# The front of a three-layer transformer kernel: weights of the first projection by feature chunk, the condition vector broadcast by its transfer, spare products ahead

## The chip, the cores and the metric

The kernel runs as one program on one core of a Trainium2 chip. A core has five engines that work side by side on one on-chip memory: TensorE (PE, matrix products into eight PSUM banks), VectorE (DVE), ScalarE (ACT), GpSimd (POOL), and SyncE (SP), which here issues all DMA transfers. The time is device microseconds of one execution; the kernel before took 1167.01 us, the median of three runs from 1165.86 to 1167.97.

## The reference

256 tokens of 1024 features pass three layers. The first two are modulated by a condition vector `c`; the front of the kernel is concerned with these lines:

```python
mod = jnp.einsum('bd,ldm->lbm', jax.nn.silu(c), w_mod) + b_mod[:, None, :]
for i in range(DEPTH):
    sh_m, sc_m, g_m, sh_f, sc_f, g_f = [t[:, None, :] for t in jnp.split(mod[i], 6, axis=-1)]
    h = x * (1.0 + sc_m) + sh_m
    if i % 2 == 0:
        y = even_mixer(h, cos, sin, w_in_even[i // 2], w_out_even[i // 2])
    else:
        ...
    x = layer_norm(ALPHA * x + (1.0 + g_m) * y, ln_mix_g[i], ln_mix_b[i])
    h = x * (1.0 + sc_f) + sh_f
    y = swiglu(h, w_gate[i], w_up[i], w_down[i])
    x = layer_norm(ALPHA * x + (1.0 + g_f) * y, ln_ffn_g[i], ln_ffn_b[i])
```

`w_mod` is 2 x 1024 x 6144, so `mod` costs 50 MB of reading, 12288 outputs in 96 chunks of 128. `even_mixer` projects `h` by `w_in_even` and runs stick-breaking attention beside a sparse attention that keeps the 64 best keys of every query (top-k over an index score); `odd_mixer` is a differential attention. The third layer is a gated linear recurrence with convolutions and a feed-forward block. All of it is fp32.

## The kernel before

Activations lie with features on the partitions: `Xf[k]` is feature chunk k (128 features x 256 tokens). Weights arrive as slabs of 1024 rows x 256 columns, in two halves of 128 x 1024. `add_plan("w0", 10, WHOLE)` lists the ten slabs of the first projection: the first seven are used as fp32 ("whole"), each half straight from its transfer into a `whi` or `wlo` buffer. All later ones are loaded into `stage`, split into two reduced-precision halves by an ACT copy (`whi`) and a DVE subtraction (`wlo`), and multiplied in three products, which together take less TensorE time than one fp32 product. `mm3` does either.

`mod_chunks(n)` handles the next chunks of `mod`: a transfer of 0.5 MB from `wmod` into an `mst` buffer (three of them; some early pairs go as one 1-MB transfer into `stage`), then one DVE scalar_tensor_tensor that multiplies with `scb` (silu(c), the same 1024 values on every partition) and adds up along the row into `raw`. After chunk pair k the DVE adds the bias, which gives shift and scale of feature chunk k, and ACT forms `Xf[k]` (L921). So the first 16 chunks gate the eight `Xf[k]`, and the first products follow k by k: `min(NST, W0 + W1 * k)` halves are in work at step k, six in all, each catching up from its chunk 0. The next two groups of 16 and 8 chunks feed the scale after the attention and the gate, which the first layer norm needs; the other chunks run beside later stages.

At the very start the vector block `vec` and the identity are loaded, ACT takes silu of the eight columns of `c`, TensorE turns their broadcasts by eight transposes (L512), and ACT copies them to `scb`. At k == 1 the rest of the constants and the positions are loaded and `rope_tables()` (L875) works out the rotary cosines and sines on DVE and ACT. Later on the path: the index scores, eight rounds of top-k on DVE, the mask `biasb`, which TensorE multiplies in by an identity; then attention, output projection, and the first layer norm, whose sums are taken by products with one column (`128x1`) and spread to all partitions by four `128x128` products with `sm`.

All operations are recorded by a `Plan`. Its `order()` simulates the engines with a cost per operation (L178) and places, on every engine and on the DMA queue, the ready operation with the lowest index plus a bias; buffers come from pools in that order. So a change in the front can move instructions anywhere. Since one helper records everything, nearly all rows of the trace carry line L428.

Of the kernel before, what the change touches and what calls it, by code (L numbers as in the profile page):

```python
# [8 lines left out]
F32 = mybir.dt.float32  # L9
# [9 lines left out]
S = 256  # L19
# [5 lines left out]
ALPHA = 4.0 ** 0.25  # L25
# [16 lines left out]
for _name, _w in (("ident", 128), ("tn", 128), ("neg1", 128), ("inv1024", 128),  # L42
                  ("causal", 128), ("strict", 128), ("inv", 1), ("sgn", 1)):
    _C[_name] = _n
    _n += _w
# [14 lines left out]
NST = 6  # L60
W0 = 1
W1 = 2
EACT = 2
WHOLE = 7
ORDER = 0
# [366 lines left out]
def kernel(ctx, tc, io, out):  # L432
# [60 lines left out]
    run.sync.dma_start(vec, io["vecs"])  # L493
    cst = const("cst", NCST)
    run.sync.dma_start(cst[:, :128], io["cst"][:, :128])
# [3 lines left out]
    def C(name, w=128):  # L499
        return cst[:, _C[name]:_C[name] + w]  # L500
# [5 lines left out]
    sc = sm("sc", 8)  # L506
    A.activation(sc, VC("c", 0, 8), AF.Silu)
    scb = const("scb", 1024)
    for i in range(2):
        ps = bank("ps_c")  # L510
        for k in range(4):
            T.transpose(ps[:, k * 128:k * 128 + 128], sc[:, 4 * i + k:4 * i + k + 1].to_broadcast([128, 128]), ident)  # L512
        A.activation(scb[:, i * 512:i * 512 + 512], ps, AF.Copy)
# [20 lines left out]
    def mod_chunks(n, lag=0):  # L534

        for _ in range(n):
# [5 lines left out]
            if 4 <= i < 16 and i % 4 < 2:  # L542
                if i % 4 == 0:
                    mod_chunks.st = run.tile("stage", SL, F32, "mst2").rearrange("p (c n) -> p c n", c=2)
                    run.sync.dma_start(mod_chunks.st, io["wmod"][i:i + 2].rearrange("c p n -> p c n"))
                st = mod_chunks.st[:, i % 4, :]
# [29 lines left out]
    add_plan("w0", 10, WHOLE)  # L576
# [334 lines left out]
    ws, pss = [], [gbank("ps_g") for _ in range((NST + 1) // 2)]  # L911
    for k in range(8):
# [3 lines left out]
        if k == 1:  # L916
            run.sync.dma_start(cst[:, 128:], io["cst"][:, 128:])
        new = len(ws)
        while len(ws) < min(NST, W0 + W1 * k):
            ws.append(take())  # L920
        A.activation(Xf[k], x0[k // 4][:, k % 4, :], AF.Identity, scale=MV(0, 1, k), bias=MV(0, 0, k))  # L921
        for c, w in enumerate(ws):
            for kk in range(0 if c >= new else k, k + 1):
                mm3(pss[c // 2][:, (c % 2) * S:(c % 2) * S + S], w, kk, X, kk, ALLT, kk == 0 and c % 2 == 0, kk == 7)
        if k == 1:
            rope_tables()
    if WHOLE < 10:
        for k in range(8):
            split(X[0][k], X[1][k], Xf[k])
    ps = bank("ps_s")  # L930
    for k in range(8):
        T.matmul(ps[:, :S], C("inv1024"), x0[k // 4][:, k % 4, :], start=k == 0, stop=k == 7)
    xm = w1("xm")[:, :S]
    A.activation(xm, ps[:, :S], AF.Copy, scale=ALPHA)
# [799 lines left out]
def lay_out(inputs):  # L1734
# [40 lines left out]
    cst[:, _C["inv1024"]:_C["inv1024"] + 128] = 1.0 / 1024  # L1775
# [84 lines left out]
```

## Time and profile before

| | us |
|---|---|
| median of three runs | 1167.01 |
| profiled execution | 1165.6 |
| its span on the core | 1163.8 |
| TensorE busy | 1132.3 (97%) |
| VectorE busy | 910.6 (78%) |
| ScalarE busy | 723.5 (62%) |

The span is what the trace covers; 1.8 us of the execution lie around it. Busy time of TensorE comes from records of passes: an fp32 product with 256 columns is two passes, so a row "x8" of these holds four products. "Granted clock" is the share of its full speed that the chip allowed TensorE, as a mean over the window; over the whole span it was 0.988.

### The profile page before, as it was taken

Reading aid. Unit: us, or ns where it says so; the run is one execution under the profiler, and the core shown is the slowest. Engines: PE = TensorE matmul, PEld = TensorE weight load, DVE = VectorE, ACT = ScalarE, POOL = GpSimd, SP = SyncE. Lnnn points to the kernel's source line nnn. Section 1 sums busy time; section 2 is a strip of 40 time slices with the busy share of each in tenths; the row PEclk is TensorE's granted clock in tenths of the full one; section 3 lists DMA queues with packets and bytes.
Section 4 is the critical chain, followed back from the end, with each engine's and each line's share of the span. In section 5 each row is a group of like instructions: output and inputs, shape, how many; then the busy total and the mean of one; then the engine's idle time right before and its main releaser. Section 6 shows DMA issues by size and latency. Waiting matters only on the chain.

```text
span 1163.8 us, 22183 instructions
## 1 busy us (share of the span) xinstructions
PE 1132.3 (97%) x8835; PEld 1083.9 (93%) x8835; DVE 910.6 (78%) x1686; ACT 723.5 (62%) x1312; POOL 88.2 (8%) x84
## 2 busy tenths in 40 slices
PE   5999999999999899999999999999999999999997
PEld 4885899999999778999999999999999999999996
DVE  6799899888999999865557886996669887866642
ACT  3558676445449887764455558786767865655541
POOL 0110200000231302000003400000000010000011
PEclk9999989999999999899999999999999999999998
DMA  9938758988995333455554634344433424555441
GB/s 353 409 131 309 240 196 319 337 325 305 335 335 191 114 129 126 145 218 184 187 191 168 228 110 158 130 148 179 155 117 131 178 87 171 195 188 193 169 163 37
DMA packets 42247, 232.28 MB, mean 200 GB/s; under 512 B 4640, under 2 KB 6176, under 8 KB 24096
## 3 DMA queue, kind: packets, MB, share of 16 engines
q1 hardware_dynamic: 42144, 230.87, 55.0%
q8 instruction: 69, 1.13, 0.4%
q14 instruction: 34, 0.28, 0.1%
HBM read 229.81 MB, written 1.05 MB: 198 GB/s over the span
## 4 chain that ended last, share of the span: by engine, by line
PE 85%; DVE 7%; DMA 3%; ACT 3%; issue 1%; DVEq 0%; SPq 0%; ACTq 0%
PE pa L428 85%; DVE w L428 4%; ACT w L428 2%; DVE wlo L428 2%; DMA mst<-in_wmod_dram 1%; DVE sm L428 1%; DVE mst L428 1%; DMA whi<-in_w_dram 1%; DMA cst<-in_cst_dram 1%; ACT whi L428 1%; DMA vec<-in_vecs_dram 0%; ACT sm L428 0%; ACT scb L428 0%; DVE lnv0lmg L428 0%; DVEq L1856 0%
## 5 line engine op out<-in xcount | busy, mean ns | idle before, releaser
L428 PE MATMUL pa<-w,whi 128*128 128x256 f32 (+4 forms) x5104 | 914.5, 287 | 9.6 <-DMA whi<-in_w_dram 7.5
L428 PEld LDWEIGHTS pa<-w,whi 128*128 128x128 f32 x5104 | 766.9, 190 | 17.0 <-ACT w L428 7.6
L428 PE MATMUL pa<-w,wlo 128*128 128x256 f32 (+3 forms) x2608 | 659.5, 289 | 0.0
L428 ACT ACTIVATE whi<-stage 128x1024 fp32r<-128x1024 f32 (+1 forms) x330 | 340.2, 1042 | 257.2 <-PE pa L428 233.9
L428 DVE TENSOR_TENSOR wlo<-stage,whi 128x1024 fp32r<-128x1024 f32 (+1 forms) x330 | 401.4, 1226 | 110.1 <-ACT whi L428 104.5
L428 PEld LDWEIGHTS pa<-w,wlo 128*128 128x128 f32 x2608 | 464.0, 190 | 7.7 <-issue 4.0
L428 ACT ACTIVATE w<-w 128x256 fp32r<-128x256 f32 (+9 forms) x257 | 117.6, 470 | 74.0 <-DVE w L428 70.3
L428 ACT ACTIVATE w<-pa 128x256 f32<-128x256 f32 (+12 forms) x298 | 108.3, 391 | 40.9 <-PE pa L428 36.1
L428 DVE TENSOR_TENSOR w<-w,w 128x256 fp32r<-128x256 f32 (+7 forms) x263 | 120.1, 474 | 8.0 <-ACT w L428 5.1
L428 DVE SCALAR_TENSOR_TENSOR mst<-mst,scb 128x1024 f32<-128x1024 f32 x90 | 109.5, 1226 | 10.8 <-DMA mst<-in_wmod_dram 10.6
L428 DVE TENSOR_TENSOR w<-w,pa 128x256 f32<-128x256 f32 (+2 forms) x146 | 58.9, 417 | 57.3 <-PE pa L428 52.3
L428 POOL TENSOR_TENSOR w<-w,w 128x256 f32<-128x256 f32 (+1 forms) x50 | 56.5, 1150 | 527.5 <-ACT w L428 320.7
L427 ACT ACT_TABLE_LOAD x59 | 75.7, 1283 | 1.7 <-PEq L1850 0.7
L428 PE MATMUL pa<-w,w 128*128 128x128 f32 (+8 forms) x340 | 70.0, 331 | 1.7 <-DVE w L428 1.1
L428 PEld LDWEIGHTS pa<-w,w 128*128 128x128 f32 (+4 forms) x340 | 41.4, 171 | 11.5 <-issue 4.1
L428 PE MATMUL pa<-cst,w 128*128 128x1 f32 (+4 forms) x284 | 46.5, 265 | 3.6 <-DVE w L428 2.2
L428 PEld LDWEIGHTS pa<-cst,w 128*128 128x128 f32 (+2 forms) x284 | 36.0, 175 | 12.0 <-ACT w L428 4.5
L428 POOL TENSOR_TENSOR w<-w 128x256 f32<-128x256 f32 x4 | 3.2, 799 | 415.2 <-DVE w L428 415.2
L428 PE MATMUL pa<-w 128*128 128x128 f32 x240 | 34.6, 274 | 0.0
L428 PE MATMUL pa<-whi,w 128*128 128x512 f32 x96 | 32.5, 417 | 0.2 <-ACT w L428 0.2
L428 PEld LDWEIGHTS pa<-w 128*128 128x128 f32 x240 | 31.2, 191 | 0.0
L428 DVE SCALAR_TENSOR_TENSOR w<-pa,vec,w 128x256 f32<-128x256 f32 (+1 forms) x48 | 23.1, 482 | 6.7 <-PE pa L428 5.7
(145 smaller groups left out, 537.1 us busy)
## 6 DMA issues: line engine op xcount, KB each, us to landing
mst<-in_wmod_dram SPq DMA_DIRECT2D x90, 512.0 KB, 5.4
stage<-in_wgu_dram SPq DMA_DIRECT2D x44, 1024.0 KB, 4.9
stage<-in_wi_dram SPq DMA_DIRECT2D x36, 1024.0 KB, 4.8
stage<-in_wup_dram SPq DMA_DIRECT2D x22, 1024.0 KB, 4.8
stage<-in_wd_dram SPq DMA_DIRECT2D x24, 896.0 KB, 4.7
stage<-in_w_dram SPq DMA_DIRECT2D x15, 1024.0 KB, 6.2
stage<-in_wo_dram SPq DMA_DIRECT2D x12, 1024.0 KB, 4.8
stage<-in_wd_dram SPq DMA_DIRECT2D x12, 1024.0 KB, 4.8
```

What stands on the lines that cost most here:

```text
L427: self.nc.scalar.preload_act_table_set(tables[i])
L428: fn(*[real(a) for a in args], **{k: real(a) for k, a in kw.items()})
```

## The change

The condition vector comes by a transfer that repeats its 4 KB on all 128 partitions (512 KB written), and ACT takes silu of the 128 x 1024 result in place; the eight transposes and two copies go. `vec` arrives in two parts, its first 104 columns early, the rest after the loop. The constants `1/1024` are set by GpSimd and no longer loaded. TensorE runs twelve fp32 products of a tile of ones into a bank that nobody reads.

The first four slabs lie in a new array `w0k` by feature chunk: at step k two transfers of 128 x 512 (256 KB each) bring the chunk's rows of all eight column blocks, and TensorE multiplies these eight with `Xf[k]`. The sums of x (`inv1024` products) are spread over the steps. The 1-MB transfers of chunk pairs move from even to odd k (four instead of three). The constants and the rotary tables move from k == 1 to k == 5.

```diff
-NST = 6
-W0 = 1
-W1 = 2
+NK = 8
+NWARM = 12
...
-    run.sync.dma_start(vec, io["vecs"])
+    scb = const("scb", 1024)
+    c_ap = io["cvec"]
+    run.sync.dma_start(scb, bass.AP(tensor=c_ap.tensor, offset=c_ap.offset, ap=[[0, 128], [1, 1024]]))
+    run.sync.dma_start(vec[:, :104], io["vecs"][:, :104])
     cst = const("cst", NCST)
-    run.sync.dma_start(cst[:, :128], io["cst"][:, :128])
+    inv1024 = const("inv1024", 128)
+    G.memset(inv1024, 1.0 / 1024)
+    wt = w2("wt")
+    V.memset(wt, 1.0)
+    ps = bank("ps_w")
+    for i in range(NWARM):
+        T.matmul(ps[:, :S], wt[:, :128], wt[:, :S], start=True, stop=True)
...
-    sc = sm("sc", 8)
-    A.activation(sc, VC("c", 0, 8), AF.Silu)
-    scb = const("scb", 1024)
-    for i in range(2):
-        ps = bank("ps_c")
-        for k in range(4):
-            T.transpose(ps[:, k * 128:k * 128 + 128], sc[:, 4 * i + k:4 * i + k + 1].to_broadcast([128, 128]), ident)
-        A.activation(scb[:, i * 512:i * 512 + 512], ps, AF.Copy)
+    A.activation(scb, scb, AF.Silu)
...
-            if 4 <= i < 16 and i % 4 < 2:
-                if i % 4 == 0:
+            if i < 16 and i % 4 >= 2:
+                if i % 4 == 2:
...
-    add_plan("w0", 10, WHOLE)
+    add_plan("w0", 10 - NK // 2, WHOLE - NK // 2)
...
-        if k == 1:
-            run.sync.dma_start(cst[:, 128:], io["cst"][:, 128:])
-        new = len(ws)
-        while len(ws) < min(NST, W0 + W1 * k):
-            ws.append(take())
+        wk = []
+        for a in range(2):
+            w = run.tile("wlo" if a else "whi", HW, F32, "whole")[:, :NK * 64]
+            run.sync.dma_start(w, io["w0k"][k][:, a * NK * 64:(a + 1) * NK * 64])
+            wk += [w[:, j * 128:j * 128 + 128] for j in range(NK // 2)]
         A.activation(Xf[k], x0[k // 4][:, k % 4, :], AF.Identity, scale=MV(0, 1, k), bias=MV(0, 0, k))
-        for c, w in enumerate(ws):
-            for kk in range(0 if c >= new else k, k + 1):
-                mm3(pss[c // 2][:, (c % 2) * S:(c % 2) * S + S], w, kk, X, kk, ALLT, kk == 0 and c % 2 == 0, kk == 7)
-        if k == 1:
+        for c in range(NK):
+            T.matmul(pss[c // 2][:, (c % 2) * S:(c % 2) * S + S], wk[c], Xf[k], start=k == 0 and c % 2 == 0, stop=k == 7,
+                     skip_group_check=True)
+        if k % 2:
+            for kk in (k - 1, k):
+                T.matmul(ps_x, C("inv1024"), x0[kk // 4][:, kk % 4, :], start=kk == 0, stop=kk == 7)
+        if k == 5:
+            run.sync.dma_start(cst, io["cst"])
             rope_tables()
+    run.sync.dma_start(vec[:, 104:], io["vecs"][:, 104:])
```

What the planner makes of it shows in the order of instructions. On VectorE before, the rotary tables (from the CAST of the positions in `w` to `cosT`) stand around the first pair of chunks from `stage`, the pair of k = 2:

```order
L428 CAST w_1_217<-w_0_201 128x256
L428 TENSOR_SCALAR w_1_217<-w_1_217,cst_100 128x256
L428 TENSOR_SCALAR w_2_224<-w_1_217 128x256
L428 TENSOR_SCALAR w_2_224<-w_2_224 128x256 x2
L428 SCALAR_TENSOR_TENSOR w_1_217<-w_2_224,w_1_217 128x256 x3
L428 TENSOR_SCALAR w_1_217<-w_1_217 128x256
L428 SCALAR_TENSOR_TENSOR stage_203,raw_185<-stage_203,scb_169 128x1024 x2
L428 TENSOR_TENSOR mod_193<-raw_185,bm_131 128x2
L428 TENSOR_TENSOR w_3_239<-w_3_239 128x256
L428 TENSOR_SCALAR cosT_262<-w_3_239 128x256
L428 CAST strib_264<-cst_100 128x128
L428 CAST causb_266<-cst_100 128x128
```

After the change they stand behind the third of these pairs, that of k = 5 (`stage_233`), and ahead of the chunks of k = 6 (`mst`):

```order
L427 SCALAR_TENSOR_TENSOR stage_233,raw_154<-stage_233,scb_101 128x1024 x2
L427 TENSOR_TENSOR mod_170<-raw_154,bm_143 128x2
L427 CAST identb_302<-cst_254 128x128
L427 CAST strib_304<-cst_254 128x128
L427 CAST causb_307<-cst_254 128x128
L427 CAST w_1_309<-w_0_261 128x256
L427 TENSOR_SCALAR w_1_309<-w_1_309,cst_254 128x256
L427 TENSOR_SCALAR w_2_314<-w_1_309 128x256
L427 TENSOR_SCALAR w_2_314<-w_2_314 128x256 x2
L427 SCALAR_TENSOR_TENSOR w_1_309<-w_2_314,w_1_309 128x256 x3
L427 TENSOR_SCALAR w_1_309<-w_1_309 128x256
L427 SCALAR_TENSOR_TENSOR mst_264,raw_154<-mst_264,scb_101 128x1024
```

With them moved the three casts of constants. Ahead of the scales for the first layer norm (`mod` with 16 columns) VectorE before runs chunks (`mst`) and evictions of products (`w<-pa,w`), and no splitting of weights:

```order
L428 SCALAR_TENSOR_TENSOR mst_1078,raw_185<-mst_1078,scb_169 128x1024
L428 SCALAR_TENSOR_TENSOR mst_1118,raw_185<-mst_1118,scb_169 128x1024
L428 SCALAR_TENSOR_TENSOR mst_1138,raw_185<-mst_1138,scb_169 128x1024
L428 TENSOR_TENSOR w_18_1062<-pa_1172,w_4_1059 128x256
L428 SCALAR_TENSOR_TENSOR w_13_1170<-pa_1030,w_13_1170 128x512
L428 SCALAR_TENSOR_TENSOR w_13_1170<-pa_1066,w_13_1170 128x256
L428 SCALAR_TENSOR_TENSOR mst_1157,raw_185<-mst_1157,scb_169 128x1024
L428 SCALAR_TENSOR_TENSOR mst_1174,raw_185<-mst_1174,scb_169 128x1024
L428 SCALAR_TENSOR_TENSOR mst_1190,raw_185<-mst_1190,scb_169 128x1024
L428 TENSOR_TENSOR mod_193<-raw_185,bm_131 128x16
```

After the change six of the subtractions that make `wlo` stand there, of the first feed-forward slabs, and the last two chunks behind or between them:

```order
L427 SCALAR_TENSOR_TENSOR mst_1199,raw_154<-mst_1199,scb_101 128x1024
L427 TENSOR_TENSOR wlo_1263<-stage_899,whi_1244 128x1024
L427 TENSOR_TENSOR wlo_1277<-stage_899,whi_1255 128x1024
L427 TENSOR_TENSOR wlo_1293<-stage_989,whi_1271 128x1024
L427 TENSOR_TENSOR wlo_1309<-stage_989,whi_1283 128x1024
L427 TENSOR_TENSOR wlo_1321<-stage_1050,whi_1299 128x1024
L427 SCALAR_TENSOR_TENSOR mst_1213,raw_154<-mst_1213,scb_101 128x1024
L427 TENSOR_TENSOR wlo_1351<-stage_1050,whi_1332 128x1024
L427 SCALAR_TENSOR_TENSOR mst_1220,raw_154<-mst_1220,scb_101 128x1024
L427 TENSOR_TENSOR mod_170<-raw_154,bm_143 128x16
```

Those six moved ahead of the scales. On TensorE before, the one-column sums of the first layer norm (`128x1`, ten rows of two, the last six here) follow each other, and products with feed-forward weights (258 columns) begin behind them:

```order
L428 MATMUL pa_1457<-cst_100,w_11_1396 128x1 x2
L428 MATMUL pa_1457<-cst_100,w_2_1424 128x1 x2
L428 MATMUL pa_1457<-cst_100,w_11_1396 128x1 x2
L428 MATMUL pa_1457<-cst_100,w_1_1455 128x1 x2
L428 MATMUL pa_1457<-cst_100,w_11_1396 128x1 x2
L428 MATMUL pa_1457<-cst_100,w_3_1476 128x1 x2
L428 MATMUL pa_1496<-w_5_1259,whi_1357 128x258
L428 MATMUL pa_1496<-w_0_1263,whi_1357 128x258
L428 MATMUL pa_1496<-w_5_1259,wlo_1382 128x258
```

After the change feed-forward products run ahead of the sums and among them:

```order
L427 MATMUL pa_1437<-w_5_1399,wlo_1321 128x258
L427 MATMUL pa_1478<-inv_0_99,w_7_1421 128x1 x2
L427 MATMUL pa_1431<-w_5_1399,whi_1271 128x258
L427 MATMUL pa_1454<-w_5_1399,whi_1332 128x258
L427 MATMUL pa_1478<-inv_0_99,w_8_1427 128x1 x2
L427 MATMUL pa_1478<-inv_0_99,w_14_1425 128x1 x2
L427 MATMUL pa_1478<-inv_0_99,w_0_1457 128x1 x2
L427 MATMUL pa_1478<-inv_0_99,w_14_1425 128x1 x2
L427 MATMUL pa_1478<-inv_0_99,w_2_1469 128x1 x2
L427 MATMUL pa_1478<-inv_0_99,w_14_1425 128x1 x2
```

So 37 of these 258-column products instead of 15 stand ahead of the four that spread the norm's results.

## Rows read from the trace of the kernel before

**Rows 1.** The page, first part: busy us, share of the span, instructions of TensorE.

```profile
PE 1132.3 (97%) x8835; PEld 1083.9 (93%) x8835; DVE 910.6 (78%) x1686; ACT 723.5 (62%) x1312; POOL 88.2 (8%) x84
```

**Rows 2.** What TensorE waited for in the span: us in total, times, longest.

```profile
PE pa L428 <- DMA whi<-in_w_dram: 7.5, 3, 4.5
```

**Rows 3.** Timeline of TensorE: start, duration, passes, idle before and its releaser.

```profile
3.33 1.95 PE L428 MATMUL pa<-cst,sm 128*128 128x128 f32 x8 [3.33 <-ACT sm L428]
9.80 1.19 PE L428 MATMUL pa<-w,whi 128*128 128x256 f32 x2 [4.52 <-DMA whi<-in_w_dram]
13.56 1.22 PE L428 MATMUL pa<-w,whi 128*128 128x256 f32 x2 [2.57 <-DMA whi<-in_w_dram]
...
49.59 3.62 PE L428 MATMUL pa<-w,wlo 128*128 128x256 f32 x16
```

**Rows 4.** Windows: busy us (x) of each engine, granted clock, DMA share, GB/s.

```profile
0.00:43.57 43.57, 30.41 (x126) 24.99 (x127) 31.01 (x106) 14.48 (x26) 1.16 (x5) 1.00 0.97 372
43.57:80.30 36.73, 34.44 (x166) 29.49 (x166) 30.48 (x93) 22.20 (x39) 9.46 (x10) 1.00 0.57 224
80.30:134.34 54.04, 53.90 (x285) 37.06 (x285) 49.13 (x100) 39.45 (x100) 0.00 (x0) 1.00 0.86 292
134.34:157.05 22.71, 21.62 (x179) 21.33 (x177) 22.40 (x44) 14.91 (x26) 6.74 (x6) 0.93 0.64 218
```

**Rows 5.** Windows: early transfers, the fall of the clock, steady work.

```profile
9.00:12.00 3.00, 1.19 (x2) 0.50 (x2) 0.00 (x0) 0.56 (x1) 0.00 (x0) 1.00 1.03 419
...
157.80:160.40 2.60, 2.60 (x14) 2.60 (x13) 2.43 (x8) 1.87 (x5) 0.00 (x0) 0.50 0.87 266
200.00:220.00 20.00, 20.00 (x171) 20.00 (x171) 17.49 (x27) 10.19 (x16) 0.00 (x0) 1.00 0.94 333
```

**Rows 6.** Timeline of VectorE in the front.

```profile
12.25 1.23 DVE L428 SCALAR_TENSOR_TENSOR mst<-mst,scb 128x1024 f32<-128x1024 f32 x1 [3.33 <-DMA mst<-in_wmod_dram]
...
17.46 0.28 DVE L428 CAST w<-w 128x256 f32<-128x256 int32 x1
...
20.74 1.22 DVE L428 SCALAR_TENSOR_TENSOR stage<-stage,scb 128x1024 f32<-128x1024 f32 x1
...
30.13 1.22 DVE L428 SCALAR_TENSOR_TENSOR stage<-stage,scb 128x1024 f32<-128x1024 f32 x1 [2.04 <-DMA stage<-in_wmod_dram]
...
43.49 0.16 DVE L428 TENSOR_TENSOR mod<-raw,bm 128x2 f32<-128x2 f32 x1
```

**Rows 7.** VectorE groups from 0 to 160 us: busy, mean ns, idle before.

```profile
L428 DVE SCALAR_TENSOR_TENSOR mst<-mst,scb 128x1024 f32<-128x1024 f32 x37 | 44.9, 1220 | 10.8 <-DMA mst<-in_wmod_dram 10.6
L428 DVE TENSOR_TENSOR wlo<-stage,whi 128x1024 fp32r<-128x1024 f32 x20 | 25.5, 1295 | 1.6 <-ACT whi L428 1.6
```

**Rows 8.** The page, fifth part: ScalarE groups, xcount | busy, mean ns.

```profile
L428 ACT ACTIVATE whi<-stage 128x1024 fp32r<-128x1024 f32 (+1 forms) x330 | 340.2, 1042 | 257.2 <-PE pa L428 233.9
...
L428 ACT ACTIVATE w<-w 128x256 fp32r<-128x256 f32 (+9 forms) x257 | 117.6, 470 | 74.0 <-DVE w L428 70.3
```

**Rows 9.** DMA issues: KB each, median us from issue to landing.

```profile
vec<-in_vecs_dram SPq DMA_DIRECT2D x1, 163.0 KB, 2.3
w<-in_pos_dram SPq DMA_DIRECT2D x1, 128.0 KB, 8.9
```

**Rows 10.** Chain of waits from 80 to 330 us: start, us, what.

```profile
115.29 6.06 DMA mst<-in_wmod_dram
...
157.05 173.03 PE pa L428 x1448
```

**Rows 11.** Timeline of TensorE at the top-k mask and the first layer norm.

```profile
80.31 0.27 PE L428 MATMUL pa<-biasb,identb 128*128 128x256 bf16 x1 [1.94 <-DVE biasb L428]
...
148.61 4.55 PE L428 MATMUL pa<-cst,w 128*128 128x1 f32 x40
...
157.05 1.11 PE L428 MATMUL pa<-cst,sm 128*128 128x128 f32 x4 [1.08 <-DVE sm L428]
```

**Rows 12.** What VectorE waited for from 43.57 to 157.05 us.

```profile
DVE mst L428 <- DMA mst<-in_wmod_dram: 3.9, 5, 1.2
```

More of the change, by code (lines that the diff above doesn't have):

```diff
@@ L41 @@
 _n = 0
-for _name, _w in (("ident", 128), ("tn", 128), ("neg1", 128), ("inv1024", 128),
+for _name, _w in (("ident", 128), ("tn", 128), ("neg1", 128),
                   ("causal", 128), ("strict", 128), ("inv", 1), ("sgn", 1)):
@@ L499, in C @@
     def C(name, w=128):
-        return cst[:, _C[name]:_C[name] + w]
+        return inv1024[:, :w] if name == "inv1024" else cst[:, _C[name]:_C[name] + w]
     def VC(name, j, w=1):
@@ L541, in mod_chunks @@
             run.bias += lag
-            if 4 <= i < 16 and i % 4 < 2:
-                if i % 4 == 0:
+            if i < 16 and i % 4 >= 2:
+                if i % 4 == 2:
                     mod_chunks.st = run.tile("stage", SL, F32, "mst2").rearrange("p (c n) -> p c n", c=2)
                     run.sync.dma_start(mod_chunks.st, io["wmod"][i:i + 2].rearrange("c p n -> p c n"))
-                st = mod_chunks.st[:, i % 4, :]
+                st = mod_chunks.st[:, i % 4 - 2, :]
             else:
@@ L910 @@
     xa = Vec8("xa", S)
-    ws, pss = [], [gbank("ps_g") for _ in range((NST + 1) // 2)]
+    pss = [gbank("ps_g") for _ in range(NK // 2)]
+    ps_x = bank("ps_s")[:, :S]
     for k in range(8):
@@ L929 @@
             split(X[0][k], X[1][k], Xf[k])
-    ps = bank("ps_s")
-    for k in range(8):
-        T.matmul(ps[:, :S], C("inv1024"), x0[k // 4][:, k % 4, :], start=k == 0, stop=k == 7)
     xm = w1("xm")[:, :S]
-    A.activation(xm, ps[:, :S], AF.Copy, scale=ALPHA)
+    A.activation(xm, ps_x, AF.Copy, scale=ALPHA)
     for k in range(8):
@@ L1774, in lay_out @@
     cst[:, _C["neg1"]:_C["neg1"] + 128] = -1.0
-    cst[:, _C["inv1024"]:_C["inv1024"] + 128] = 1.0 / 1024
     cst[:, _C["causal"]:_C["causal"] + 128] = np.where(i[None, :] <= i[:, None], 0.0, NEG)
@@ L1816, in lay_out @@
     sb, v, qd = slabs(np.concatenate([q_sb, k_sb], axis=1)), tok_slabs(v_sb), slabs(qd)
-    res["w0"] = np.concatenate([a, *((qd, sb, v), (sb, v, qd), (sb, qd, v))[ORDER]])
+    w0 = np.concatenate([a, *((qd, sb, v), (sb, v, qd), (sb, qd, v))[ORDER]])
+    n = NK // 2
+    res["w0k"] = w0[:n].reshape(n, 128, 2, 8, 128).transpose(3, 1, 0, 2, 4).reshape(8, 128, n * 256)
+    res["w0"] = w0[n:]
+    res["cvec"] = f["c"].reshape(1024)
     wo = f["w_out_even"][0]
```

## The prediction

> **What bounds the kernel now.** I read the page's first part, then what TensorE waited for, then windows of the front. TensorE is busy for 1132.3 of the span's 1163.8 us [rows 1], so 31.5 us of idle time are all that better overlap can win. The longest entry is 7.5 us for the first weights, three waits [rows 2], and all of it lies early: 4.52 us before the pass at 9.80, 2.57 before that at 13.56 [rows 3], the rest later. In the front TensorE works 30.41 of the first 43.57 us [rows 4]. Up to 80.30 its longest gap is 1.94 us before the top-k mask [rows 11], and from there it works 53.90 of 54.04 and 21.62 of 22.71 us [rows 4].
>
> But TensorE does not alone set when the stages end. Followed back from 157.05, the chain of waits goes through VectorE and through the transfers of modulation chunks (6.06 us at 115.29), and from 157.05 it is 173 us of TensorE without a break [rows 10]. So the first layer norm, at 157.05, is the gate: what the change wins ahead of it counts as far as that moment moves, and then as work left over behind it. VectorE is busy 30.48 + 49.13 + 22.40 = 102.0 of the 113.5 us before that gate [rows 4]: 11.5 us idle, of which 3.9 wait for modulation chunks [rows 12].
>
> **Head and broadcast.** Eight transposes (1.95 us, [rows 3]) and two ACT copies go, and a 512-KB transfer with an ACT silu of 128 x 1024 come; by the copies of that size the silu is 1.04 us [rows 8]. The transfer is not in the trace. The fast neighbour is `vec`, 163 KB in 2.3 us at the same place, first in the queue; the slow one is the other transfer that repeats a row, the positions, 8.9 us for 128 KB, but behind other transfers [rows 9]. I take 3 to 5 us, nearer to the first since nothing stands ahead of it; at the slow end everything in the queue comes some 4 us later. Whatever the first chunk pair loses there VectorE has slack for: it idles 3.33 us before the chunk at 12.25 and 2.04 before the pair at 30.13 [rows 6]. What counts is when the bytes come. The twelve spare products run while TensorE would wait; slow ones (0.6 us a pass at 9.80, [rows 3]) would be 24 x 0.6 = 14 us and push step 0 back to about 15 us, which the later steps absorb, since each chunk pair, weights and x (1.05 + 0.52 + 0.13 MB) needs 4.1 us at 419 GB/s [rows 5], and TensorE 3.9 us (below). Cost 0, bound +2.
>
> **The eighth feature chunk.** Before, its scales are there at 43.6 [rows 6]. After, the queue has carried 10.28 MB through the pair of k = 5; before, the pair that lands at 30.13 [rows 6] had 10.13 MB with it. The difference is 0.15 / 0.419 = 0.4 us later, less about 1 us for the head, in which fewer small transfers stand: 29.5 (28.9 to 31). Behind that, VectorE's row is full, as the order shows: the pair and its bias 2.5; three casts 0.4; the first part of the rotary tables 3.3 (17.46 to 20.74, [rows 6]); a chunk 1.15; cosine 0.7; a chunk 1.25; with bias and residual terms 2.2; the last pair 2.4. Sum 13.9, so 43.4 to 43.6, with the bounds 42.8 to 45. Before, the tables lay in time in which VectorE waited for transfers; now they lie on its path, and they eat what the earlier weights could have won. Gain at the eighth chunk: 0.
>
> **TensorE to the mask.** A pass of 256 columns takes 3.62 / 16 = 0.226 us with its tail, 0.215 pitch [rows 3], a product 0.43; a step has eight and one for the sums of x: 3.9 us. The last step starts at 44.1 (ACT needs 0.47 for 128 x 256, [rows 8]) and ends near 47.7. What then stands ahead of the first mask product, counted in the order: 48 fp32 products x 0.43 = 20.6, 43 split ones x 0.117 (20.00 / 171, [rows 5]) = 5.0, transposes and index products 3.7: 29.3, so 77.0, against 80.31 before [rows 11]. 20 of the split products are new there (2.3 us of later work). VectorE's top-k chain ends about then as well: 1.6 us of its work has left the stretch; I take the mask at 78.
>
> **The gate.** TensorE's own floor: 78 + 53.9 + 21.6 + 2.6 (22 feed-forward products of 0.117 more ahead of the norm, as the order shows) - 2.3 (the 20 done earlier) - 1.1 (half clock in the last stretch, mean 0.93, [rows 4]) = 152.7. VectorE's: 43.6 + 113.5, plus 2.3 for the operations that the order moves ahead of the gate (one chunk of 1.22 and one subtraction of 1.3, [rows 7], less small ones), less the idle time that it wins back. Of that I take 3.9 [rows 12] and 1.1 before its first eviction, 5.0, since weights and chunks are loaded a little earlier; bounds 0, and 9.7, where TensorE's floor stops it. Gate: 154.4, 2.6 us earlier.
>
> Behind it TensorE has 2.6 us less to do, because of the pulled products. Against that VectorE has two more chunks left in the second layer (2.4 us), where it is as loaded as TensorE; I charge 1.0 of it, bounds 0 and 2.4. Sum: -2.6 - 2.6 + 1.0 = -4.2. The profiled execution took 1165.6 (1163.8 and 1.8 around it), 1.4 below the median of 1167.0. So 1161.4 in its terms and 1162.8 in those of the median.
>
> **Rivals.** *TensorE's floor decides (B).* The steps of VectorE that I count as path are filled in elsewhere and the gate falls to 152.7: -4.4 - 2.6 + 0 = -7.0, 1160. For it: TensorE is at 53.90 of 54.04 in the middle stretch [rows 4]. Against it: VectorE at 49.13, with chunks that its own queue holds up [rows 10].
>
> *The clock falls between the steps (C).* The front becomes eight bursts of 3.5 us with gaps of 1.3 to 3 us (from the times above: the sixth step ends at 37, the seventh starts at 39.4 and the eighth at 44.1). In the trace a gap of 1.94 us [rows 11] left the granted clock at full speed, whereas the passes behind gaps of 4.52 and 2.57 us took twice their later time [rows 3], and in the gate of the layer norm, behind 40 one-column passes and a gap of 1.08, it stands at 0.50, which is 1.2 of 2.4 GHz [rows 5, 11]. Slow seventh and eighth steps cost up to 3.4 us each: mask at 80 to 82.6, gate near 157, and with the pulled products 1166 (1165 to 1168), no change to the sum that the rest would notice. By the Trainium skill (TensorE: Matmul & The Clock Gate, HAM oscillation) bursts that wait for transfers can start cold each time, also where each is short against its wait; here each burst is longer than its gap, and no stretch of this trace has such a pattern, so it keeps a chance of its own and does not enter the sum.
>
> *VectorE pays in full (D), slower.* The mechanism is the place of the rotary tables and of the subtractions ahead of the scales: if none of the 11.5 us of idle time is won back, the gate is 43.6 + 113.5 + 2.3 = 159.4, with a late pair of k = 5 at 160.8; +2.4 to +3.8, less 2.6, and the second layer's +2.4 in full: +2.2 to +3.6, 1169 to 1170.6. It decides from the point where VectorE's idle time between the eighth chunk and the norm stays above about 10 us. For it: most of these waits are for results of other engines, which come when they come, and transfers take 0.86 of the time there [rows 4]. Against it: mask and first projections come about 2 us earlier.
>
> That the change doesn't do what it says (the weights not earlier, TensorE not busier by 40 us) I give no chance of its own: by bytes, the first 64 products have their weights at hand.
>
> **Chances and range.** Forecast 0.52, with its own range 1160 to 1165.5; B 0.14; C 0.15; D 0.19. A measurement of this kernel tells about 0.2%, 2.3 us, from no change. Faster by more: most of the forecast (0.45) and B, 0.59. Within: the rest of the forecast, C, and the mild end of D, 0.24. Slower: 0.17. The range reaches from below B, 1156.5, which also holds a clock that does not fall at the norm, to D's lower end, 1169.5; unlikelier ends lie outside.
>
> **What would show it.** Right: the eighth chunk's bias at 43 to 45 with the tables directly ahead of it on VectorE; the first mask product near 78; the spreading products of the first norm between 153 and 156; TensorE idle some 4 us less after 50 us than before. Wrong: passes of 0.4 us or more after 25 us (C); the norm at 157 or later (D) or the eighth chunk earlier than 42, which would mean that VectorE was not its bound; and a gain at the norm that is gone by the second layer's end, since the two chunks left over stand there.

## The result and the profile after

The changed kernel takes 1174.33 us (median, 1170.29 to 1179.85), the kernel before 1167.01; the ratio is 1.0059, with a 95% interval from 1.0043 to 1.0076. It is 7 us slower, and 1162.8 was forecast. One more run took 1237.9 us at a granted clock of 0.84 and is left out as slow. The profiled execution took 1175.77 us, 10.2 more than that of before, so some 3 us of what the two traces show between them are not in the medians. The page:

```profile
span 1174.0 us, 22237 instructions
...
PE 1140.1 (97%) x8851; PEld 1093.1 (93%) x8851; DVE 911.2 (78%) x1687; ACT 719.5 (61%) x1308; POOL 86.2 (7%) x85
```

TensorE is busy 7.8 us longer than before [rows 1]; some 7 us of that are the twelve spare products, and the eight transposes (1.95 us) have gone. It is idle 33.9 us where it was 31.5. In stages that end where those of [rows 4] end, at the eighth chunk's bias, the first mask product, the scales and the first layer norm (busy time of PE, PEld, DVE, ACT and POOL, then granted clock, DMA share, GB/s):

```profile
0.00:44.83 44.83, 36.16 (x147) 29.62 (x148) 29.70 (x85) 11.39 (x20) 1.30 (x6) 0.97 0.98 369
44.83:81.00 36.17, 34.77 (x176) 30.11 (x175) 29.23 (x100) 22.16 (x40) 8.46 (x10) 0.99 0.51 201
81.00:147.80 66.80, 62.99 (x367) 47.30 (x367) 58.23 (x107) 44.99 (x106) 0.00 (x0) 0.97 0.79 285
147.80:164.57 16.77, 15.26 (x99) 14.45 (x98) 15.73 (x42) 8.95 (x22) 4.99 (x6) 0.81 0.49 192
```

The eighth chunk is ready at 44.83 (43.57 before), the mask at 81.00 (80.31), the scales at 147.8 (134.34), the norm's spreading products start at 164.57 (157.05): 7.5 us later, where 2.6 earlier was forecast. VectorE is busy 29.23 + 58.23 + 15.73 = 103.2 us of the 119.7 behind the eighth chunk: 16.5 us idle, 11.5 before. So the 7.5 us are 1.3 from the front, 1.2 of more work and 5.0 of more idle time on the engine that I had taken for the path.

VectorE in the front (start, duration, operation, idle before with its releaser), which answers to [rows 6]:

```profile
6.32 1.23 DVE L427 SCALAR_TENSOR_TENSOR mst<-mst,scb 128x1024 f32<-128x1024 f32 x1 [0.46 <-DMA mst<-in_wmod_dram]
...
30.23 1.23 DVE L427 SCALAR_TENSOR_TENSOR stage<-stage,scb 128x1024 f32<-128x1024 f32 x1 [0.43 <-DMA stage<-in_wmod_dram]
...
33.49 0.23 DVE L427 CAST identb<-cst 128x128 bf16<-128x128 f32 x1 [0.68 <-DMA cst<-in_cst_dram]
...
37.19 1.22 DVE L427 SCALAR_TENSOR_TENSOR mst<-mst,scb 128x1024 f32<-128x1024 f32 x1
...
44.75 0.16 DVE L427 TENSOR_TENSOR mod<-raw,bm 128x2 f32<-128x2 f32 x1
```

The first chunk is multiplied at 6.32 (5.95 before). The broadcast took 4.0 us from issue to landing, inside the 3 to 5 forecast, and was no gain:

```profile
scb<-in_cvec_dram SPq DMA_DIRECT2D x1, 512.0 KB, 4.0
```

The pair of k = 5 comes at 30.23, and the rotary tables do stand between it and the next chunk, at 37.19, as the order had shown. The constants they need land late, 0.68 us after VectorE is free for them.

TensorE in the front: 22 of the 24 passes of spare products run at 0.3 us a pass (the last two follow at 10.31), and the seventh step waits 2.84 us for ScalarE's activation and then runs slowly, 2.71 and 2.90 us for eight passes against 1.89 in the eighth step:

```profile
1.45 6.60 PE L427 MATMUL pa<-w 128*128 128x256 f32 x22 [1.45 <-DVE w L427]
...
41.10 2.71 PE L427 MATMUL pa<-w,whi 128*128 128x256 f32 x8 [2.84 <-ACT w L427]
43.60 2.90 PE L427 MATMUL pa<-w,wlo 128*128 128x256 f32 x8
46.35 1.89 PE L427 MATMUL pa<-w,whi 128*128 128x256 f32 x8
```

Further on, TensorE at the mask, in attention and at the norm's one-column sums, ScalarE's operand for the eviction behind the second wait, and VectorE around that wait and ahead of the norm:

```profile
81.00 0.38 PE L427 MATMUL pa<-biasb,identb 128*128 128x256 bf16 x2 [1.41 <-DVE biasb L427]
...
117.03 3.53 PE L427 MATMUL pa<-w,cst 128*128 128x512 f32 x6 [3.81 <-DVE w L427]
...
155.87 5.67 PE L427 MATMUL pa<-inv,w 128*128 128x1 f32 x36
```

```profile
113.47 0.58 ACT L427 ACTIVATE w<-pa 128x512 fp32r<-128x512 f32 x1
```

```profile
113.86 1.23 DVE L427 SCALAR_TENSOR_TENSOR mst<-mst,scb 128x1024 f32<-128x1024 f32 x1 [1.31 <-DMA mst<-in_wmod_dram]
...
115.14 1.22 DVE L427 SCALAR_TENSOR_TENSOR mst<-mst,scb 128x1024 f32<-128x1024 f32 x1
...
116.29 1.02 DVE L427 SCALAR_TENSOR_TENSOR w<-pa,w 128x512 f32<-128x512 f32 x2
...
147.74 0.17 DVE L427 TENSOR_TENSOR mod<-raw,bm 128x16 f32<-128x16 f32 x1
...
159.87 1.22 DVE L427 SCALAR_TENSOR_TENSOR mst<-mst,scb 128x1024 f32<-128x1024 f32 x1
...
161.01 1.22 DVE L427 SCALAR_TENSOR_TENSOR mst<-mst,scb 128x1024 f32<-128x1024 f32 x1
...
162.16 1.22 DVE L427 SCALAR_TENSOR_TENSOR mst<-mst,scb 128x1024 f32<-128x1024 f32 x1
...
163.31 0.15 DVE L427 COPY sm<-pa 128x4 f32<-128x4 f32 x1
```

Read them together: TensorE waits 3.81 us for an eviction (`w<-pa,w` at 116.29). Its operand from ScalarE is there at 114.05, but two modulation chunks stand ahead of it on VectorE, the first of them waiting itself for its transfer. The scales follow at 147.74, and from 159.87 three more chunks stand ahead of the COPY that takes the norm's sums. The sums end at 161.54, so the COPY at 163.31 comes 1.8 us later than it could; TensorE does not wait there, it runs feed-forward products. In the second layer TensorE waited before and after for (us in total, times, longest; from 355 to 495 us, first before, then after):

```profile
PE pa L428 <- DVE w L428: 3.7, 5, 1.6
PE pa L428 <- ACT w L428: 2.2, 4, 1.4
```

```profile
PE pa L427 <- DVE w L427: 5.1, 5, 1.9
PE pa L427 <- DVE wlo L427: 2.8, 3, 1.4
PE pa L427 <- DVE sm L427: 1.1, 1, 1.1
PE pa L427 <- ACT whi L427: 0.4, 1, 0.4
```

The waits for `wlo` are new. And behind gaps the granted clock is low (5-us windows of the changed kernel):

```profile
40.00:45.00 5.00, 3.90 (x12) 3.20 (x13) 4.93 (x15) 2.36 (x4) 0.00 (x0) 0.72 1.04 409
115.00:120.00 5.00, 2.97 (x7) 1.73 (x7) 4.21 (x11) 0.26 (x1) 0.00 (x0) 0.73 0.90 333
390.00:395.00 5.00, 3.12 (x23) 2.95 (x22) 4.77 (x11) 4.19 (x16) 2.19 (x2) 0.88 0.08 30
480.00:485.00 5.00, 3.92 (x18) 3.62 (x19) 4.39 (x13) 0.82 (x2) 0.00 (x0) 0.50 0.98 383
```

The first of these lies behind the gap of 2.84 us, the second around that of 3.81, the third at a wait of 1.88 us; in the kernel before, none of these three stretches is below 1.00. The fourth lies at the first layer norm of the second layer, where the kernel before falls to 0.50 as well (from 475 to 480 us). Full speed is 2.4 GHz, so 0.50 is 1.2 GHz. The whole span's mean is 0.982 (0.988 before); over the runs it is 0.977 to 0.989 for the changed kernel, and the runs of 1170.3 and 1170.7 us are those at 0.987 and 0.989, those of 1178 to 1180 at 0.977 to 0.979. Runs of the kernel before, beside the experiments, go from 0.982 (1171 us) to 0.992 (1163). At one and the same clock of 0.987 the two differ by some 3 us (the one run of the changed kernel there took 1170.3, those of the kernel before 1167.2 in the mean); the rest goes along with the lower clock.

### The profile page after: what moved, and what is told of

It reads as the page before. It is cut to its first block, busy times and chain, and to the rows that moved or that the text cites. A ratio compares the mean times of both kernels' runs of the same rounds, so it can differ in the third digit from the quotient of the medians.

```text
span 1174.0 us, 22237 instructions
## 1 busy us (share of the span) xinstructions
PE 1140.1 (97%) x8851; PEld 1093.1 (93%) x8851; DVE 911.2 (78%) x1687; ACT 719.5 (61%) x1308; POOL 86.2 (7%) x85
## 4 chain that ended last, share of the span: by engine, by line
PE 81%; DVE 9%; DMA 4%; ACT 4%; issue 1%; POOL 0%; SPq 0%; DVEq 0%; ACTq 0%; POOLq 0%
PE pa L427 81%; DVE w L427 4%; DMA mst<-in_wmod_dram 3%; ACT w L427 3%; DVE wlo L427 2%; DVE mst L427 2%; DVE sm L427 1%; ACT whi L427 1%; DMA cst<-in_cst_dram 1%; POOL w L427 0%; SPq L427 0%; ACT sm L427 0%; DVEq L1863 0%; DVE cosT L427 0%; DVE mod L427 0%
## 5 line engine op out<-in xcount | busy, mean ns | idle before, releaser
L427 DVE SCALAR_TENSOR_TENSOR mst<-mst,scb 128x1024 f32<-128x1024 f32 x88 | 106.2, 1220 | 3.9 <-DMA mst<-in_wmod_dram 3.4
L427 PE MATMUL pa<-w 128*128 128x128 f32 (+1 forms) x264 | 41.9, 292 | 1.5 <-DVE w L427 1.5
L427 PEld LDWEIGHTS pa<-w 128*128 128x128 f32 x264 | 37.0, 196 | 2.5 <-DVE w L427 1.5
L427 PE MATMUL pa<-cst,w 128*128 128x128 f32 (+2 forms) x122 | 25.6, 275 | 3.9 <-DVE w L427 3.9
L427 POOL TENSOR_TENSOR w<-w,sinT 128x512 f32<-128x512 f32 (+1 forms) x14 | 18.4, 1316 | 109.7 <-ACT w L427 84.8
```

What stands on the lines that cost most here:

```text
L427: fn(*[real(a) for a in args], **{k: real(a) for k, a in kw.items()})
```

## The experiments

Three theories at first. TABLES: the rotary tables ahead of the eighth chunk cost the time. ORDER: what the planner then put where, ahead of the norm and in the second layer, costs it. CLOCK: the front's gaps let the clock fall. Each ratio is to runs of the kernel before on the same chip, with its 95% interval.

**Without the spare products.**

```diff
-NWARM = 12
+NWARM = 0
```

> The changed kernel with NWARM = 0: no spare products, the order of everything else on all engines the same. Theory ORDER (the planner put six subtractions and a chunk more ahead of the scales of the first norm, which delays the norm): nothing there changes, so as the changed kernel, 1172 to 1176. Theory CLOCK (the front's bursts and gaps let the clock fall, and that costs the time): the first steps run at 0.6 us a pass, +6 us at step 0, which later steps absorb; but the fall of the clock at about 41 us stays, so also 1172 to 1176, and if the spare products were what brings the clock up and its later fall with it, passes at 41 us change. Theory HEAD (the spare products push the first step back): 1 to 2 us faster.

1175.45 us, ratio 1.0068 (1.0045 to 1.0092): as the changed kernel. The spare products neither cost nor bring anything that can be measured. One of the five runs took 1168.61 us, at a granted clock of 0.987; the trace is of that run.

**Tables at k == 1.**

```diff
-        if k == 5:
+        if k == 1:
             run.sync.dma_start(cst, io["cst"])
             rope_tables()
```

> The changed kernel with constants and rotary tables at k == 1 again. Theory TABLES (they lie on VectorE's path in front of the eighth chunk): the eighth chunk's bias falls from 44.75 to 42.3 to 43.3 us, where the transfers hold it; the gap of 2.84 us before the seventh step shrinks below 1 and the slow passes at 41 us go (1.9 us); the norm 2 to 3 us earlier, time 1170 to 1172. Theory ORDER: 15 subtractions still stand between mask and scales as in the changed kernel, so whatever is won at the eighth chunk waits again; norm within 1.5 us of 164.6, time 1172 to 1175.

1167.62 us, ratio 1.0005 (0.9993 to 1.0016): the whole loss is gone. The eighth chunk's bias on VectorE, and there TABLES was right:

```profile
43.36 0.16 DVE L427 TENSOR_TENSOR mod<-raw,bm 128x2 f32<-128x2 f32 x1
```

But the norm still comes at 163.84, as ORDER had it, and the time is better than either theory said. The edit also shifted the order behind the front, so by itself it does not tell them apart.

**LAG = 200, after and before.** LAG is what the planner adds to the index of the modulation chunks behind the front, so that they come later in the order; the edit lets them come earlier.

```diff
-LAG = 300
+LAG = 200
```

> The changed kernel with LAG = 200 for 300: the front stays instruction for instruction, but the chunks of the first norm come earlier in the planner's priority: 9 subtractions instead of 15 between mask and scales, none of the three chunks between scales and norm, 15 feed-forward products ahead of the norm instead of 37. Theory ORDER: scales back to 134 to 138 us (147.7 in the changed kernel), norm at 156 to 159, time 5 to 8 us less than the changed kernel, 1166 to 1169. Theory TABLES or CLOCK: front the same, so the norm moves by less than 2 us and the time stays 1172 or more.

1169.62 us, ratio 1.0039 (1.0018 to 1.0061): 4.7 us less than the changed kernel by the medians, 2.3 by the ratios, with the same front; the intervals overlap, and the time is above ORDER's range and below that of the others. Scales at 137.27, and the norm, on TensorE, as ORDER had it:

```profile
158.64 0.65 PE L427 MATMUL pa<-cst,sm 128*128 128x128 f32 x4 [1.63 <-DVE sm L427]
```

> The kernel before with LAG = 200: the control for the constant itself. It moves two chunks from behind the mask to ahead of it and leaves the rest nearly as it was. ORDER: as the kernel before, 1165 to 1169, mask up to 2 us later. If the constant alone were a gain, 1162 or less, and the run before it would not speak for ORDER.

1169.61 us, ratio 1.0021 (1.0005 to 1.0037): the constant alone makes the kernel before slower, by 2 to 3 us. So it is no gain of its own; and an order can cost that much without any change in the work.

**Both edits.** Tables at k == 1 and LAG = 200.

> The changed kernel with the tables at k == 1 and LAG = 200, that is both edits that helped alone (tables at k == 1: 6.7 us less than the changed kernel, norm still at 163.8; LAG 200: 4.7 less, norm at 158.6). In the order 9 subtractions stand between mask and scales, none of the three chunks behind, 12 feed-forward products ahead of the norm. If the two causes are separate (TABLES in the front, ORDER ahead of the norm) the gains add up: norm at 155 to 158, 1162 to 1165, faster than the kernel before. If both edits act by one thing, the order that they happen to give to the second layer and the clock, they do not add: 1166 to 1169.

1169.02 us, ratio 1.0015 (1.0003 to 1.0027). They do not add, although the norm starts 5 us earlier than with the tables alone (158.69). An early norm is no gain by itself: what TensorE has done ahead of it may count as much, which was not tested alone.

**Six spare products in the gap.**

```diff
             rope_tables()
+            ps_f = bank("ps_f")
+            for i in range(6):
+                T.matmul(ps_f[:, :S], inv1024, Xf[5], start=True, stop=True)
```

> The changed kernel with six more spare products behind the sixth step (they need Xf[5]), in the gap of 2.84 us before the seventh. Tables stay at k == 5; but the planner's order behind the front comes out with the same counts as with the tables at k == 1 (46 chunks in the stretch behind the first norm and 8 in the second layer, for 44 and 9). Theory TABLES: the eighth chunk stays at 44.7, time 1172 to 1176. Theory CLOCK: the seventh step runs at full clock (1.89 us for eight passes instead of 2.7 to 2.9), 2 to 4 us less, 1170 to 1172, granted clock 0.985 or more. Theory ORDER in the second layer: the waits for subtractions at 369 to 374 us (2.8 us) go as they did with the tables at k == 1, time 1167 to 1170.

1167.1 us, ratio 0.9996 (0.9986 to 1.0006). This ends TABLES: the tables stand where the change put them, the eighth chunk comes at 45.09, later than in the changed kernel, and yet nothing is lost. The seventh step (second row) now follows the spare products at full speed:

```profile
38.17 3.62 PE L427 MATMUL pa<-w,inv 128*128 128x256 f32 x16
41.63 1.89 PE L427 MATMUL pa<-w,whi 128*128 128x256 f32 x8
```

That leaves two causes in one edit, the filled gap and the order that came with it.

**One at a time.** The next two kernels take them apart. In the first the planner sees the six products, but they are not issued: every other instruction of every engine stands as in the kernel above. In the second they are issued but count nothing for the planner: the order is that of the changed kernel, instruction for instruction.

```diff
+            if any("ps_f" in nm for nm in ops[i][6]):
+                continue
```

> The kernel with six spare products behind the sixth step (1167.1), with the same order of every other instruction on every engine, but these six not run: the gap before the seventh step is open again. If the order is what made that kernel 7 us faster than the changed one, it stays at 1166.5 to 1168.5, with the front's fall of the clock back (1.9 us at the seventh step, part of it hidden). If the filled gap and the clock did it, 1171 to 1176.

```diff
+        if writes and "ps_f" in writes[0].name:
+            cost, work = 0.0, 0.0
```

> The other half: the changed kernel's order, instruction for instruction on all engines, with the six spare products run behind the sixth step. If the order decides, the waits of the changed kernel stay (idle 4 to 5.5 us between mask and norm, 9 us in the second layer, the wait of about 3.8 us near 115) and the time is 1171 to 1175. If the clock of the front decides, the seventh step at full clock brings 1166.5 to 1169.

| median us (ratio, interval) | gap open | gap filled |
|---|---|---|
| order of the changed kernel | 1174.33 (1.0059, 1.0043 to 1.0076) | 1172.56 (1.0046, 1.0029 to 1.0063) |
| the other order | 1168.29 (1.0016, 0.9998 to 1.0034) | 1167.10 (0.9996, 0.9986 to 1.0006) |

By the medians the order makes 5.5 to 6 us and the gap 1.2 to 1.8; by the ratios, each to runs on its own chip, 5.0 to 5.8 and 1.5 to 2.3. The order's intervals stand apart in both columns. The gap's overlap in both rows, so its share is not shown, though both differences have the same sign. The seventh step of the second kernel is at full speed (first row). But so it is in one kernel with the front of the changed one and the gap open, the exchange of evictions below (second row), while five other traces with the gap open have it slow:

```profile
41.24 1.99 PE L429 MATMUL pa<-w,whi 128*128 128x256 f32 x8 [0.27 <-ACT w L429]
```

```profile
41.11 1.99 PE L440 MATMUL pa<-w,whi 128*128 128x256 f32 x8 [2.25 <-ACT w L440]
```

Where the order costs it: windows between mask and norm, and in the second layer, first of the order of the changed kernel with the gap filled, then of the other order, with the gap filled as well (PE busy is the first figure behind the length, the clock the third from the end):

```profile
81.00:170.00 89.00, 84.55 (x499) 68.25 (x498) 77.37 (x158) 58.30 (x135) 4.97 (x6) 0.90 0.73 266
355.00:495.00 140.00, 130.54 (x901) 118.15 (x900) 129.11 (x297) 111.20 (x275) 21.66 (x18) 0.95 0.42 151
```

```profile
81.00:170.00 89.00, 85.61 (x534) 69.64 (x533) 81.88 (x170) 62.64 (x144) 4.94 (x6) 0.96 0.74 266
355.00:495.00 140.00, 135.04 (x942) 120.50 (x941) 133.16 (x303) 118.88 (x289) 22.58 (x18) 0.98 0.39 140
```

Idle 4.5 against 3.4 us and 9.5 against 5.0, and the clock 0.90 against 0.96 and 0.95 against 0.98. So 5.6 us less waiting, 4.5 of it in the second layer. The waits go with the order: without the first spare products, in a run of 1168.61 us, the changed kernel's order has 4.4 and 10.4 us. The clock does not do so clearly: that run has 0.94 and 0.98, and of the two traces here the first is of a run of 1176.66 us, 4 above the median of its kernel, the other of one of 1165.99, 1 below.

The same shows in when the norms' spreading products start:

| us | before | changed | its order, gap filled | other order, gap filled |
|---|---|---|---|---|
| first norm | 157.05 | 164.57 | 165.63 | 161.01 |
| second norm | 350.85 | 354.50 | 355.48 | 352.14 |
| third, behind the second layer's attention | 477.83 | 484.62 | 485.57 | 478.26 |
| end of the span | 1163.8 | 1174.0 | 1174.9 | 1163.9 |

From the second norm to the third the changed kernel's order takes 130.1 us in both traces, the kernel before 127.0, the other order 126.1.

**Single places of that order.** With the causes still spread over two stretches, two exchanges in the changed kernel's order, nothing else moved but the loads into the buffers concerned. First the evictions behind the wait of 3.81 us, ahead of the two chunks:

```diff
-chunk, chunk, eviction, eviction   (VectorE, 113.86 to 117.3 us)
+eviction, eviction, chunk, chunk
```

> The changed kernel with one exchange in VectorE's order: the two evictions of a stick-breaking product that TensorE waits for 3.81 us before 117.03 stand ahead of the two modulation chunks, not behind them; the loads into these two buffers move along. ScalarE delivers their operand at about 114.1, so they can start there and not at 116.3. If that wait is a cause of the loss: TensorE's wait falls to 1 to 2 us, the fall of the clock at 115 to 125 goes, and the time is 1170 to 1172.5 (the changed kernel: 1174.3, the same with the gap in the front filled 1172.6). If the stretch ahead of the norm is bound by VectorE anyway, the two chunks come 1 us later there, the wait is given back before the norm at 164.6, and the time stays 1173.5 to 1175.5.

1171.18 us, ratio 1.0033 (1.0022 to 1.0045), 3 us less than the changed kernel by the medians, though the intervals touch. TensorE's long wait became two short ones, the clock from 115 to 125 us is full, and the norm moved from 164.57 to 162.94:

```profile
114.03 1.99 PE L440 MATMUL pa<-w,cst 128*128 128x512 f32 x6 [1.12 <-DVE w L440]
117.25 0.51 PE L440 MATMUL pa<-w,whi 128*128 128x256 f32 x2 [1.23 <-DVE w L440]
```

This does not show that the wait made 3 us. Traces with the order unchanged reach the norm between 161.75 us (without the first spare products) and 165.63 (gap filled), and the wait itself is 2.07 and 2.93 us in these two, so 162.94 lies within what one order gives.

In the second layer two chunks behind the subtractions that TensorE waits for:

```diff
-chunk, product, split, ..., chunk, ..., split, ..., split   (VectorE, 366 to 375 us)
+product, split, chunk, ..., split, ..., split, chunk
```

> The changed kernel with two modulation chunks of the second layer moved behind subtractions that TensorE waits for (at 369.25, 370.30 and 374.16 us, 2.8 us in all); everything else in order, one load exchanged with a slab's. If these waits are a cause of the loss: they fall below 1 us, the second layer's idle time of 9.5 us comes near 7, and the time is 1171 to 1172.5. If the mixer's chain on VectorE bounds that stretch whatever stands where, the idle time only moves to the waits for w at 383 and 393, and the time stays 1173.5 to 1175.5.

1171.13 us, ratio 1.0042 (1.0023 to 1.0061), which does not separate from 1.0059, though the median is 3 us lower here too. The waits, from 355 to 495 us, in the trace of a run of 1177.49 us:

```profile
PE pa L451 <- DVE w L451: 5.1, 5, 2.4
PE pa L451 <- DVE sm L451: 2.0, 1, 2.0
PE pa L451 <- ACT whi L451: 1.4, 1, 1.4
PE pa L451 <- DVE wlo L451: 0.9, 2, 0.7
```

Those for `wlo` fell from 2.8 to 0.9 us as meant, those for `sm` and `whi` grew from 1.5 to 3.4: together 9.4 as before. So moving these two chunks only moved the waits about. That a chain on VectorE bounds the stretch, the second theory, fits this, though neither its time nor the places that it named came out; it was not tested further. What the better order does there in all was not taken apart further.

**Parts and sizes.** The head alone on the kernel before (broadcast, silu of 128 x 1024, vec in two parts, no transposes, no spare products):

> The kernel before with the new head alone: condition vector broadcast by its transfer, silu on 128 x 1024, vec in two parts, no transposes; slabs, chunk transfers, tables and identity as before, no spare products. The trace of the changed kernel shows the first chunk multiplied at 6.32 us instead of 5.95, so the head wins nothing for the chunks; TensorE loses 1.95 us of cold transposes that nobody waits for. Every theory: 1165 to 1168, no change; a gain of 2 us or more would mean that the transposes mattered, a loss of as much that the split of vec (256 packets under 512 bytes more) or the broadcast costs the transfers.

1171.41 us, ratio 1.0040 (1.0026 to 1.0054), against every theory. The first chunk is multiplied at 7.29 us for 5.95, the eighth chunk's bias came at 44.74 for 43.49, the norm at 164.34: here the head does delay the front, by 1.3 us. Here too the order behind the front changed (between the first two norms the trace has 50 chunks for 49), so this does not say that the broadcast as such costs 4 us; it was not tried with the order held. The kernels with the same head at 1167.1 and 1167.62 us lose nothing, so if it costs anything there, the rest of the change gains as much.

Three slabs by chunk instead of four, tables at k == 1:

```diff
-NK = 8
+NK = 6
```

> The changed kernel with tables at k == 1 and three slabs by chunk instead of four (NK = 6): 1 MB less ahead of the eighth chunk, 2.5 us at 0.41 MB/us. The planner's order behind it has nearly the counts of the kernel before (9 subtractions between mask and scales, 16 feed-forward products ahead of the norm, 47 and 7 chunks). TABLES (time set by the eighth chunk): its bias at 40.5 to 41.5, norm 2 to 3 us earlier than before, 1164 to 1165. ORDER: like the kernel before with a slightly better front, 1164 to 1167. If TensorE's work in the front is what counts, it has a quarter less of it at hand per step, 1166 to 1169.

1168.06 us, ratio 1.0002 (0.9987 to 1.0018). The eighth chunk came at 41.44, 2 us before the kernel before, the norm at 158.34, and nothing was won: TensorE was idle for 8.8 us up to 45 and for 5.8 from 81 to 170 us. An earlier eighth chunk is worth nothing by itself.

Tables at k == 1, spare products behind the first and the sixth step, LAG = 250, as a version to beat both:

> A try for a version faster than both: tables at k == 1, spare products behind the first and the sixth step, LAG = 250 (12 subtractions between mask and scales, 4 behind, 46 and 7 chunks in the second layer's stretches). If idle time and clock falls add as the runs so far show (front idle 4 to 6, no fall before 81 us, second layer idle 5 to 6), 1163 to 1166; if the order ahead of the norm costs as in the other runs (idle 3.5 to 5 between mask and norm, where the kernel before has 1.2), 1166 to 1168.

1166.18 us, ratio 0.9995 (0.9975 to 1.0014): faster than the changed kernel by 8 us, the same as the kernel before. No version beat that.

## Why the prediction was wrong

**Head: right for the transfer, not clear for the cost.** The broadcast took 4.0 us, the first chunk came 0.4 us later than before, the spare products were free. By the head alone the eighth chunk came 1.3 us later, and the credit of "about 1 us for the head" in the next term did not appear: the pair of k = 5 came 0.1 us behind the 30.13 of before, not 0.6 ahead.

**The eighth chunk: right in kind, 1.3 us off.** The pair of k = 5 came at 30.23 for 29.5 and the constants 0.68 us late; 44.75 lies inside the bounds of 42.8 to 45, and traces of the same order give 43.97 to 45.31. But the weight that I put on it, in the sum and in the reason for D, was wrong: with it at 45.09 a kernel took 1167.1 us, with it at 41.44 1168.1.

**The mask: 81.0 for 78.** I let TensorE's products set it. They did not, before or after: the first mask product waited 1.94 us for VectorE before [rows 11] and 1.41 after, TensorE's products ended at 79.6 (77.0 forecast), and VectorE's chain from the eighth chunk to the mask took 36.2 us (44.83 to 81.00) as it had taken 36.7 (43.57 to 80.31). The slow seventh step, C's mechanism, cost 1.8 us of TensorE (2.71 + 2.90 against twice 1.89) but nothing at the mask, which comes at 80.85 with the gap filled. By the section HAM oscillation of the Trainium skill (TensorE: Matmul & The Clock Gate) bursts that wait for a transfer can start cold. The step here waited for ScalarE, and the traces agree with the "can": behind the gap of 2.84 us it ran slowly, behind one of 2.25 us in the exchange of evictions at full speed, and with the gap filled at full speed. In the whole kernel the gap made 1.2 to 1.8 us by the medians, which is not clear of noise.

**The gate: the step that failed.** The term was VectorE's 159.4, less the idle time that it wins back, 5.0 us. It came out as 5.0 us more idle time, and the norm at 164.57 for 154.4. (The bound of 9.7 was wrong as well: TensorE's floor of 152.7 stops it at 6.7.) I reasoned that earlier weights and an earlier mask let waits shrink, and counted the subtractions and chunks that the order moves ahead of the gate only as work, 2.3 us (measured: 1.2). What they also did was stand in front of results on the path, which VectorE takes in its order: the chunks at 113.86 and 115.14 ahead of an eviction that was ready at 114.05, the three at 159.87 ahead of the COPY of the norm's sums, 1.8 us too late. How much of the 5.0 us each of them made is not shown. Rows 12 show the 3.9 us of waits for chunks, but no row showed that they would go, and 2.9 were left; VectorE's waits for ScalarE's results (`w`, `whi`) rose from 4.1 to 7.9 us.

That the norm was the gate of the kernel was wrong in part too. With the tables at k == 1 it came at 163.84 and the time was that of the kernel before; with the norm at 158.69 it was 1169.02.

**Behind the gate.** From the norm to the second norm the changed kernel takes 354.50 - 164.57 = 189.9 us for 350.85 - 157.05 = 193.8: 3.9 us less, 2.6 forecast, so the pulled products were work saved there. But pulled ahead of the mask and the norm they were also what would have filled the waits between them: idle time from 81 to 170 us is 5.3 for 1.2 us.

**The second layer: the other term that failed, 1.0 charged, 3.1 to 3.6 measured.** From the second norm to the third the changed kernel takes 3.1 us more. Idle time from 355 to 495 us, worked out from these windows of before and after:

```profile
81.00:170.00 89.00, 87.78 (x551) 70.65 (x550) 81.93 (x171) 64.67 (x149) 6.74 (x6) 0.96 0.75 255
355.00:495.00 140.00, 134.09 (x925) 120.13 (x924) 129.09 (x292) 115.76 (x283) 21.07 (x18) 0.96 0.37 132
```

```profile
81.00:170.00 89.00, 83.69 (x508) 67.17 (x508) 78.44 (x161) 59.05 (x137) 4.99 (x6) 0.94 0.72 266
355.00:495.00 140.00, 130.52 (x899) 118.17 (x899) 128.84 (x294) 111.07 (x274) 21.69 (x18) 0.95 0.41 149
```

5.9 us before, 9.5 after. I took the two chunks left over as VectorE work beside an equally loaded TensorE. The waits for splits are new, but moving these chunks behind the splits left the sum of the waits as it was, so what in the order makes them stays open. Behind the third norm the two traces drift apart by another 3.4 us; some 3 us of their difference are not in the medians.

**The clock.** I put no new fall of it into the sum and gave that a chance of 0.15 as a thing of the front alone. It fell at later waits too, and some 4 of the 7 us go along with it: at 0.987 the changed kernel lies some 3 us above the one before, in the median 7. Whether the lower clock follows from the waits alone is not shown.

So D's sign was right and its mechanism half: VectorE paid, by where operations stand and not by how many there are or by the tables' place, and the time lies 3.7 us beyond D's upper end of 1170.6. That the order makes 5 to 6 of the 7 us, with most of the waiting in the second layer, is shown by the pair of orders. That single places in it make the loss is not: neither exchange separates from the changed kernel. What the head alone costs, and what lowers the clock, stays open.

## What to carry to other kernels

Where a planner sets the order, an edit in one place is a new order everywhere, and that alone made 5 to 6 us here, and 2 to 3 in the kernel before by one constant. Before a gain or loss is put down to the edit, hold the order and switch the edit, and hold the edit and switch the order. And ask of every operation that an edit moves on an engine not only how long it takes but whose result stands behind it. One trace per kernel is one execution: here the same order gave a wait of 2.07, 2.93 or 3.81 us at one place.

## What the runs showed of the hardware

The granted clock of a run goes closely with its time: over the changed kernel's runs 0.977 to 0.989 goes with 1178 to 1171 us, as wide a spread as the loss itself. In its trace the clock fell behind waits of 2.84 and 3.81 us and near one of 1.88 in the second layer.

A gap of one length gave either clock. Before the seventh step five traces with the gap open (2.2 to 2.9 us) ran it at 2.7 to 3.6 us for its first eight passes, one (2.25 us) at 1.99; both traces with six products (some 2.6 us) in the gap ran at full speed there. Behind the gap of 2.1 us before the second step the changed kernel kept the clock (1.99 us for eight passes), and the kernel with six spare products behind the sixth step did not (2.40).

A transfer that repeats 4 KB on 128 partitions, first in the queue, took 4.0 us in the changed kernel and 4.6 with the new head alone. With it the first chunk was multiplied at 6.32 us in the changed kernel and at 7.29 with the head alone, where small transfers and eight transposes had given 5.95.
